# Reordered ends of the feed forward stages in a two-layer encoder on one core

## The chip, the cores and the metric

The kernel runs on one core of a Trainium2 chip. The metric is device time in microseconds (us) of one execution, the median of several runs. A core has a matmul engine (TensorE, PE in the rows; its weight loads are PEld), a vector engine (VectorE, DVE), a scalar engine (ScalarE, ACT), a general engine (GpSimd, POOL) and a sync engine (SyncE, SP) that issues most of the DMAs. Each takes its instructions in the order in which the program lists them and waits on semaphores. Matmul results land in PSUM, in banks that are reused; everything else sits in SBUF, 128 partitions wide.

## The reference, cut to what matters

The model is a two-layer bidirectional encoder of width 1024 over two request groups of 512 and 256 tokens, which the kernel holds together as 768 tokens. Each layer is a half feed forward stage, an attention mixer, and another half feed forward stage; a norm ends the whole.

```python
def _rmsnorm(x, g):
    xf = x.astype(jnp.float32)
    y = xf * lax.rsqrt(jnp.mean(xf * xf, axis=-1, keepdims=True) + NORM_EPS)
    return (y * g.astype(jnp.float32)).astype(x.dtype)

def _swiglu(h, wg, wu, wd):
    return (jax.nn.silu(h @ wg) * (h @ wu)) @ wd          # 1024 -> 2752 -> 1024
...
    for i in range(DEPTH):                                 # DEPTH = 2
        x = x + 0.5 * _swiglu(_rmsnorm(x, norm_ffn1[i]), ffn1_wg[i], ffn1_wu[i], ffn1_wd[i])
        h = _rmsnorm(x, norm_mix[i])
...
        x = x + 0.5 * _swiglu(_rmsnorm(x, norm_ffn2[i]), ffn2_wg[i], ffn2_wu[i], ffn2_wd[i])
    return _rmsnorm(x, final_norm)
```

## The kernel before, in words

The stages follow each other: feed forward (the first, to about 535 us), the mixer of layer 0, feed forward (the second, about 974 to 1486 us), feed forward (the third, 1486 to 1997 us), the mixer of layer 1, and the last feed forward stage (about 2369 us to the end). The first and the third stage hand over to a mixer, the second to the third.

Precision is kept by splitting every operand into a high and a low part, so that one product is three matmuls (`mm3h`: high times high, low times high, high times low). The activations stay transposed: `x` holds eight rows of 128 features (`j`) by 768 tokens, in two halves of 384 tokens.

**The up part** (`ffn_up`) computes gate and up projections. It starts with a leftover: three units for the first half of the tokens (`unit(0, i)`, 24 matmuls of 384 columns each, operands b11 and b21) and three for the second (`unit(1, i)`, operands b12 and b22). The second half needs its norm first. For that `rstd_cols` sums the squares `ss` by three small matmuls (L337), VectorE and GpSimd make the reciprocal root (L270, L271), and `norm_half` spreads it with two matmuls on a diagonal (`diag`, L354) and normalizes rows on VectorE (L310, then the low parts b12l and b22l at L307). These are placed by hand between the matmuls of the first half. Twenty tiles `t` follow, each a fast block scheme of seven products; `act_up` (L646) reads the last tile's PSUM.

**The down part** (`ffn_down`) is also seven products in a block scheme, in the order `DOWN = (1, 4, 5, 6, 7, 2, 0, 3)`; 0 stands for `rest(0)`, the leftover rows of the hidden width done the plain way for half of the tokens (40 matmuls), product 3 follows it, and then `rest(1)` closes the stage. A product has five quarters `q` of 24 matmuls. Its activations come from a queue `tu`: loaded from DRAM (`traw`, SyncE), cast to `th` on ScalarE (L766), and `tl` made as the difference on VectorE (L768); the tiles of all three come from one ring of nine. The weights come through a queue `gu` in the same way (`guh` on ScalarE L375, `gul` on VectorE L379; the leftover rows' at L184 and L189). `fetch(n)` has n loads on their way; `push(i, phases)` runs the cast, and with all phases the difference too, for the i-th operand in the queue; `ahead(0)` and `ahead(1)` do so in each quarter.

When a product has its sum in PSUM, `add` (L800, VectorE) takes two rows of it into `x`. In `rest` each finished row is handed on by `done(j, q)`: for a mixer `spread` (h_hi on ScalarE L277, h_lo on VectorE L278), for a next feed forward stage nothing of that, and for both `square` (ScalarE L285 or L288, summed into `ss` on VectorE L289) and `spill`, a DMA of the row on ScalarE's queue (L292). In the second stage `after` also runs parts of the third stage's norm within product 3 and `rest(1)`. In the last stage there is no `done`; `final` (`leave`) transposes a tile of 128 tokens back (L897), squares it on ScalarE (L900), gets the reciprocal root (L270, L271), multiplies by the gain on VectorE (L902), scales on ScalarE (L904) and sends it out (L905).

PSUM of the down part is a pool with tags `x` and `y`, two buffers each of two banks. Products 1, 6 and 7 build on one chain of two `y` buffers.

All of this is scheduled by hand: the order of the code is the order on each engine. The lines

```python
            if q == 0:
                tu.fetch(3)
            gu.fetch(1)
```

at the head of `rest`, and `ahead`, decide when operands are loaded and split relative to the adds and the rows handed on.

Of the kernel before, what the change touches and what calls it, by code (L numbers as in the profile page):

```python
# [17 lines left out]
KT = D // P  # L18
# [3 lines left out]
TT = T // P  # L22
# [113 lines left out]
class Kernel:  # L136
# [406 lines left out]
    def ffn_up(self, F, cpool, psp, gain, jobs):  # L543
        nc = self.nc
        x = self.xn
# [10 lines left out]
        def unit(q, i, ks=range(KT), ps=None):  # L556
            wh, wl = us[i]
            ps = ps or psum()
            for k in ks:
                w = slice(k * P, (k + 1) * P)  # L560
                bh, bl = (t[:, k % 4] for t in comb[f"b{k // 4 + 1}{q + 1}"])
                self.mm3h(ps[:, :TH], wh[:, w], wl[:, w], bh, bl, k == 0, k == KT - 1)
            return ps
# [22 lines left out]
        ps0 = [unit(0, 0)]  # L586
        if self.has_rc:
            self.norm_half(1, st, gain)
            ps0 += [unit(0, 1), unit(0, 2)]
        else:  # L590
            self.rstd_cols(st, range(TT // 2, TT), exact=False)
            ps = unit(0, 1, range(KT - 1))
            self.norm_half(1, st, gain)
            ps0.append(unit(0, 1, range(KT - 1, KT), ps))
            ps0.append(unit(0, 2))
        ps1 = [unit(1, i) for i in range(3)]
        prep0(0)
        sub(b(1, 1), b(1, 2), b(1, 1))
# [85 lines left out]
        with ExitStack() as cx:  # L684
            for t in range(self.NS):
                y, bb, c = psum(), psum(), psum()
# [97 lines left out]
    def ffn_down(self, F, ctx, done, after, final):  # L784
        nc = self.nc
        gu, tu, x = self.gu, self.tu, self.x
        NQ = self.NS // 4
        F.stash = ctx.enter_context(self.pool("stash", side=self.other()))
        psp = ctx.enter_context(self.psum_pool("dps", 2))
        new = lambda tag: psp.tile([P, 1024], F32, tag=tag, name=tag)  # L790
        def reload(i, q):
            for r, c in {1: [(0, 0)], 4: [(1, 0)], 5: [(1, 1), (0, 1)]}.get(i, []):
                if q < 4:
                    nc.sync.dma_start(out=x[:, 4 * r + q, HALVES[c]], in_=self.xscr[4 * r + q][:, HALVES[c]])

        def add(ps, js, c, w=TH, per=512):
            n = len(js)
            v = ps.rearrange("p (b c) -> p b c", c=per)[:, :n, :w]
            xs = x[:, js[0]:js[0] + n, c]
            nc.vector.scalar_tensor_tensor(out=xs, in0=v, scalar=0.5, in1=xs, op0=ALU.mult, op1=ALU.add)  # L800

        def ahead(part):
            if part == 0:
                tu.push(0)
                gu.push(1, 2)
                gu.push(2, 2)
                tu.fetch(2)
                gu.fetch(1)
            else:
                gu.push(1)  # L810
                tu.push(0)
                tu.push(1, 1)

        def product(i, banks, first):
            for q in range(NQ):
                (wh, wl), (th, tl) = gu.get(), tu.get()
                ahead(0)
                reload(i, q)
                if i == 1 and q < self.RAW:
                    a = F.stash.tile([P, 1024], F32, name=f"A{q}")  # L820
                    nc.scalar.copy(out=a, in_=F.A[q])
                    F.A[q] = a
                for j in range(4):
                    out = banks[j // 2][:, j % 2 * 512:j % 2 * 512 + TH]
                    for m in range(2):
                        w, c = slice(512 * m + P * j, 512 * m + P * j + P), slice(TH * m, TH * m + TH)
                        self.mm3h(out, wh[:, w], wl[:, w], th[:, c], tl[:, c], first and q + m == 0, q + m == NQ, not first)
                    if j % 2:
                        if q + 1 == NQ:
                            for r, c in self.ADDS[i]:  # L830
                                add(banks[j // 2], [4 * r + j - 1, 4 * r + j], HALVES[c])
                        if j == 1:
                            ahead(1)
                            yield 2 * q
                yield 2 * q + 1

        def rest(q):
            (wh, wl), (sh, _) = gu.get(), gu.get()
            (ah, al), (bh, bl) = tu.get(), tu.get()
            if q == 0:  # L840
                tu.fetch(3)
            gu.fetch(1)
            if q and final is not None:
                for i in range(TT // 2, TT):
                    ps = new("x")
                    c = slice(i * P - TH, i * P - TH + P)
                    for j in range(KT):
                        w, o = slice(j * P, (j + 1) * P), ps[:, j * P:(j + 1) * P]
                        self.mm3h(o, wh[:, w], wl[:, w], ah[:, c], al[:, c], True, False)
                        self.mm3h(o, sh[:, w], None, bh[:, c], bl[:, c], False, True)  # L850
                    add(ps, range(KT), slice(i * P, (i + 1) * P), P, P)
                    final(i, new("y"))
                return
            for j0 in range(0, KT, 2):
                ps = new("yyxx"[j0 // 2] if q == 0 else "xxyy"[j0 // 2])
                for j in (j0, j0 + 1):
                    w, o = slice(j * P, (j + 1) * P), ps[:, (j - j0) * 512:(j - j0) * 512 + TH]
                    self.mm3h(o, wh[:, w], wl[:, w], ah[:, :TH], al[:, :TH], True, False)
                    self.mm3h(o, sh[:, w], None, bh[:, :TH], bl[:, :TH], False, True)
                add(ps, (j0, j0 + 1), HALVES[q])  # L860
                if q and j0 == 2 and after is not None:
                    after(10, None)
                if j0 == 0:
                    gu.push(0)
                    gu.push(1, 2)
                    tu.push(0)
                elif j0 == 4:
                    gu.push(1)
                    gu.push(2, 2)
                if done is not None:  # L870
                    done(j0, q)
                    done(j0 + 1, q)
        chain = [new("y") for _ in range(2)]
        for i in self.DOWN:
            if i == 0:
                rest(0)
                continue
            banks = chain if i in (1, 6, 7) else [new("y" if i == 3 else "x") for _ in range(2)]
            for q in product(i, banks, i not in (6, 7)):
                if i == 3:  # L880
                    if final is not None:
                        if q in (3, 5, 7):
                            final((q - 3) // 2, new("x"))
                    elif after is not None:
                        after(q, lambda: new("x"))
        rest(1)

    def open_final(self, ctx, out):
# [1179 lines left out]
```

## Time and profile before

| | us |
|---|---|
| median of 3 timed runs | 2906.72 (2906.03 to 2907.74) |
| the profiled execution | 2897.25 |
| its span in the trace | 2895.2 |
| PE busy | 2724.2 (94%) |
| VectorE busy | 1985.8 (69%) |
| ScalarE busy | 1302.9 (45%) |

PE is the engine to look at: it is busy for nearly the whole span. What can be read is where it is not, and where the granted clock fell to half. In a row of a timeline the start is in us from the span's start, then the duration, engine, line, operation, output and inputs, and in brackets the idle time ahead of it and what ended that. Matmuls overlap, so the distance of two starts, not the duration, tells what one costs.

### The profile page before, as it was taken

What the parts mean: (1) busy time and instruction counts of PE and PEld (TensorE: products, weight loads), DVE (VectorE), ACT (ScalarE), POOL (GpSimd) and SP (SyncE); (2) the same over time, 40 slices, a digit from 0 to 9 for tenths busy, and PEclk for the clock granted to TensorE, in tenths of its full rate; (3) what the DMA queues carried; (4) which work ended last, traced back from release to release, by engine and by line L of the source; (5) the groups of instructions that cost most, each with busy time, mean ns of one, the idle gap of its engine ahead of it and who ended that gap; (6) DMA issues with size and microseconds to landing.
All of it is one profiled execution on the core that took longest, in us unless ns stands there. A gap on an engine that the chain in (4) does not pass through costs nothing. (4 is left out here: it accounts for less than half of the span.)

```text
span 2895.2 us, 41957 instructions
## 1 busy us (share of the span) xinstructions
PE 2724.2 (94%) x16118; PEld 2653.8 (92%) x16118; DVE 1985.8 (69%) x2902; ACT 1302.9 (45%) x2130; POOL 291.0 (10%) x428
## 2 busy tenths in 40 slices
PE   6999999998989999999989999998986899999997
PEld 6999998898978999999989999997985799999997
DVE  6777678454775676767887666686775558766684
ACT  4443344454675333334443333444566524333443
POOL 0000000032242000000000000000564400000000
PEclk9999999899999999999999999998998999999998
DMA  5474466358874243446534443654334243444652
GB/s 141 122 193 128 131 240 193 106 143 248 271 233 122 62 117 114 122 132 231 180 115 114 119 119 120 241 175 137 98 122 164 93 152 89 122 119 122 243 190 86
DMA packets 415656, 432.10 MB, mean 149 GB/s; under 512 B 34208, under 2 KB 353376, under 8 KB 414432
## 3 DMA queue, kind: packets, MB, share of 16 engines
q1 hardware_dynamic: 401632, 410.55, 46.8%
q10 hardware_dynamic: 13824, 18.88, 1.8%
q8 instruction: 126, 2.06, 0.3%
q14 instruction: 74, 0.61, 0.1%
HBM read 303.60 MB, written 125.76 MB: 148 GB/s over the span
## 5 line engine op out<-in xcount | busy, mean ns | idle before, releaser
L375 ACT CAST guh<-raw 128x1024 fp32r<-128x1024 f32 (+1 forms) x220 | 229.5, 1043 | 300.3 <-DVE raw L517 216.0
L379 DVE TENSOR_TENSOR gul<-raw,guh 128x1024 fp32r<-128x1024 f32 (+1 forms) x220 | 267.3, 1215 | 12.0 <-ACT guh L375 12.0
L477 PE MATMUL y<-th,guh 128*128 128x384 f32 x696 | 237.9, 342 | 21.0 <-ACT th L766 15.1
L477 PE MATMUL y<-tl,guh 128*128 128x384 f32 x696 | 237.0, 341 | 4.9 <-DVE tl L768 4.9
L477 PE MATMUL y<-th,gul 128*128 128x384 f32 x668 | 226.6, 339 | 0.0
L768 DVE TENSOR_TENSOR tl<-traw,th 128x768 fp32r<-128x768 f32 (+1 forms) x156 | 142.5, 914 | 92.9 <-ACT th L766 85.5
L477 PE MATMUL x<-tl,guh 128*128 128x384 f32 (+1 forms) x584 | 195.7, 336 | 6.1 <-DVE tl L768 6.1
L477 PE MATMUL x<-th,guh 128*128 128x384 f32 (+1 forms) x584 | 195.2, 336 | 1.8 <-DVE guh L184 1.8
L640 ACT COPY ap<-ps 128x384 f32<-128x384 f32 x160 | 77.0, 481 | 244.7 <-PE ps L477 244.6
L477 PE MATMUL x<-th,gul 128*128 128x384 f32 (+1 forms) x532 | 178.8, 336 | 0.0
L930 PE MATMUL pj<-guh,h_hi 128*128 128x256 f32 x576 | 168.8, 293 | 3.1 <-DVE x L800 3.0
L271 POOL TENSOR_TENSOR rc<-ms,expo 128x3 f32<-128x3 f32 (+1 forms) x10 | 10.2, 1015 | 1556.1 <-DVE ms L270 1556.1
L934 PE MATMUL pj<-guh,h_lo 128*128 128x256 f32 x576 | 166.2, 288 | 0.0
L933 PE MATMUL pj<-gul,h_hi 128*128 128x256 f32 x576 | 165.0, 287 | 0.0
L477 PEld LDWEIGHTS y<-th,guh 128*128 128x128 f32 x696 | 132.2, 190 | 24.7 <-ACT th L766 16.1
L477 PEld LDWEIGHTS y<-tl,guh 128*128 128x128 f32 x696 | 132.2, 190 | 7.0 <-DVE tl L768 7.0
L477 PE MATMUL ps<-b11l,guh 128*128 128x384 f32 x368 | 127.3, 346 | 7.3 <-DVE b11l L307 7.3
L766 ACT CAST th<-traw 128x768 fp32r<-128x768 f32 (+1 forms) x156 | 124.3, 797 | 20.4 <-DMA traw<-tq 14.0
L1051 POOL TENSOR_SCALAR p<-p,sm 128x256 f32<-128x256 f32 (+1 forms) x192 | 117.8, 625 | 137.6 <-DVE sm L1048 110.5
L477 PE MATMUL ps<-o,guh 128*128 128x384 f32 x512 | 131.2, 337 | 0.0
L646 DVE TENSOR_TENSOR act<-ps,g 128x384 f32<-128x384 f32 x80 | 44.6, 558 | 124.5 <-PE ps L477 118.9
L375 ACT CAST guh<-C 128x1024 fp32r<-128x1024 f32 x60 | 63.1, 1052 | 146.6 <-DVE C L450 96.7
(332 smaller groups left out, 8528.3 us busy)
## 6 DMA issues: line engine op xcount, KB each, us to landing
traw<-tq SPq DMA_DIRECT2D x140, 384.0 KB
raw<-in_ffn_wg_dram SPq DMA_DIRECT2D x84, 512.0 KB
raw<-in_ffn_wd_dram SPq DMA_DIRECT2D x80, 512.0 KB
rawu<-in_ffn_wu_dram SPq DMA_DIRECT2D x76, 512.0 KB
tq<-tl SPq DMA_DIRECT2D x80, 384.0 KB
xscr<-x ACTq DMA_DIRECT2D x96, 192.0 KB
tq<-act SPq DMA_DIRECT2D x40, 384.0 KB
x<-xscr SPq DMA_DIRECT2D x64, 192.0 KB
```

Of the source, the lines that this page charges most:

```text
L271: nc.gpsimd.tensor_tensor(out=self.rc[:, a:b], in0=ms[:, a:b], in1=self.expo[:, a:b], op=ALU.pow)
L375: self.nc.scalar.copy(out=hi, in_=raw)
L379: self.nc.vector.tensor_tensor(out=u[1], in0=raw, in1=f32(u[0]), op=ALU.subtract)
L477: mm = nc.tensor.matmul(out, w, x, start=start and n == 0, stop=stop and n == len(pairs) - 1, skip_group_check=more)
L640: nc.scalar.copy(out=c, in_=ps[:, :TH])
L646: tt(out=act[:, 0], in0=y[:, :TH], in1=g[:, 0], op=ALU.mult)
L766: nc.scalar.copy(out=th[:, :n], in_=t[:, :n])
L768: nc.vector.tensor_tensor(out=tl[:, :n], in0=t[:, :n], in1=f32(th[:, :n]), op=ALU.subtract)
L930: m = nc.tensor.matmul(out, self.h[:, k, s], wh[:, c], start=k == 0, stop=False)
L933: nc.tensor.matmul(out, self.h[:, k, s], wl[:, c], start=False, stop=False)
L934: nc.tensor.matmul(out, self.l[:, k, s], wh[:, c], start=False, stop=k == KT - 1)
L1051: nc.gpsimd.tensor_scalar(out=pt[:, c], in0=pt[:, c], scalar1=sm[:, 2 + s:3 + s], scalar2=1.0, op0=ALU.mult, op1=ALU.mult)
```

## The change

It alters five things, all in the feed forward stages.

1. In `ffn_up`, where the norm's reciprocal was not made beforehand (second, third and last stage), `rstd_cols` moves behind 12 more matmuls, and `norm_half` behind 9 more; the first half still ends at the same count of matmuls, so 18 instead of 27 stand between `norm_half` and the second half.
2. `ahead` gets the number of quarters left in products 2 and 3. With one left three loads are kept on their way instead of two; in the last quarter the second operand ahead is split in full (`tu.push(1, 9)`, so its `tl` too) before the second add.
3. `rest(0)` pushes the second activation operand of product 3 before its last add, and hands rows on later: two are kept back in a queue `late`, and the last two are handed on inside product 3.
4. The two `x` buffers of product 4 are taken before the chain's `y` buffers, so the chain lies in other banks.
5. In the last stage's `rest(1)` the transposes of a tile come after the matmuls of the next one.

```diff
@@ ffn_up
         else:
+            ps = unit(0, 1, range(KT // 2))
             self.rstd_cols(st, range(TT // 2, TT), exact=False)
-            ps = unit(0, 1, range(KT - 1))
+            ps0.append(unit(0, 1, range(KT // 2, KT), ps))
+            ps = unit(0, 2, range(2))
             self.norm_half(1, st, gain)
-            ps0.append(unit(0, 1, range(KT - 1, KT), ps))
-            ps0.append(unit(0, 2))
+            ps0.append(unit(0, 2, range(2, KT), ps))
@@ ffn_down
-        def ahead(part):
+        def ahead(part, left=9):
...
-                tu.fetch(2)
+                tu.fetch(3 if left == 1 else 2)
...
-                tu.push(1, 1)
+                tu.push(1, 9 if left == 0 else 1)
...
+                left = NQ - 1 - q if i in (2, 3) else 9
+                ahead(0, left)
...
-                            ahead(1)
+                            ahead(1, left)
@@ rest, with final
-                for i in range(TT // 2, TT):
+                for i in range(TT // 2, TT + 1):
+                    if i == TT:
+                        final(i - 1, new("y"))
+                        break
...
-                    final(i, new("y"))
+                    if i > TT // 2:
+                        final(i - 1, new("y"))
@@ rest, without
+                if q == 0 and j0 == 6:
+                    tu.push(1)
                 add(ps, (j0, j0 + 1), HALVES[q])
...
-                    done(j0, q)
-                    done(j0 + 1, q)
+                    late.extend((j0, j0 + 1))
+                    while len(late) > (0 if q else 2):
+                        done(late.popleft(), q)
+        late = deque()
+        spare = [new("x") for _ in range(2)]
         chain = [new("y") for _ in range(2)]
...
-            banks = chain if i in (1, 6, 7) else [new("y" if i == 3 else "x") for _ in range(2)]
+            banks = chain if i in (1, 6, 7) else spare if i == 4 else [new("y" if i == 3 else "x") for _ in range(2)]
...
                 if i == 3:
+                    if late:
+                        done(late.popleft(), 0)
```

VectorE in `rest(0)` of the first stage, from the end of the third block of rows on: L800 (L801 after) is an add, L278 and L289 are h_lo and ss of a row handed on, L379 is a weight's low part, L768 (L769 after) is the `tl` of a quarter of product 3. Before:

```order
L800 SCALAR_TENSOR_TENSOR x<-x 128x2x384
L278 SCALAR_TENSOR_TENSOR h_lo<-x,g_norm_mix_302,h_hi 128x384
L289 TENSOR_TENSOR ss<-ss,sq 128x384
L278 SCALAR_TENSOR_TENSOR h_lo<-x,g_norm_mix_302,h_hi 128x384
L289 TENSOR_TENSOR ss<-ss,sq 128x384
L768 TENSOR_TENSOR tl<-traw,th 128x768
L379 TENSOR_TENSOR gul<-A_3344,guh 128x1024
L768 TENSOR_TENSOR tl<-traw,th 128x768
```

After:

```order
L769 TENSOR_TENSOR tl<-traw,th 128x768
L801 SCALAR_TENSOR_TENSOR x<-x 128x2x384
L278 SCALAR_TENSOR_TENSOR h_lo<-x,g_norm_mix_302,h_hi 128x384
L289 TENSOR_TENSOR ss<-ss,sq 128x384
L278 SCALAR_TENSOR_TENSOR h_lo<-x,g_norm_mix_302,h_hi 128x384
L289 TENSOR_TENSOR ss<-ss,sq 128x384
L379 TENSOR_TENSOR gul<-A_3346,guh 128x1024
L278 SCALAR_TENSOR_TENSOR h_lo<-x,g_norm_mix_302,h_hi 128x384
L289 TENSOR_TENSOR ss<-ss,sq 128x384
L278 SCALAR_TENSOR_TENSOR h_lo<-x,g_norm_mix_302,h_hi 128x384
L289 TENSOR_TENSOR ss<-ss,sq 128x384
L769 TENSOR_TENSOR tl<-traw,th 128x768
```

The first `tl` (quarter 1 of product 3) moved from behind the last add and its rows to ahead of that add; four rows' h_lo and ss, where there were two, now stand between it and the `tl` of quarter 2.

PE at the start of the second stage, where the row sums (L337) stand among the first half's matmuls; ps_10047 is the PSUM of `unit(0, 0)`, ps_10078 (ps_10072 after) that of `unit(0, 1)`. Before:

```order
L477 MATMUL ps_10047<-b21h_9441,guh_10029 128x384
L477 MATMUL ps_10047<-b21l_9442,guh_10029 128x384
L477 MATMUL ps_10047<-b21h_9441,gul_10030 128x384
L337 MATMUL ps_10046<-ones2_71,ss_9447 128x2 x3
L477 MATMUL ps_10078<-b11h_9439,guh_10035 128x384
L477 MATMUL ps_10078<-b11l_9440,guh_10035 128x384
L477 MATMUL ps_10078<-b11h_9439,gul_10036 128x384
```

After:

```order
L477 MATMUL ps_10072<-b11h_9439,guh_10035 128x384
L477 MATMUL ps_10072<-b11l_9440,guh_10035 128x384
L477 MATMUL ps_10072<-b11h_9439,gul_10036 128x384
L337 MATMUL ps_10046<-ones2_71,ss_9447 128x2 x3
L477 MATMUL ps_10072<-b21h_9441,guh_10035 128x384
L477 MATMUL ps_10072<-b21l_9442,guh_10035 128x384
L477 MATMUL ps_10072<-b21h_9441,gul_10036 128x384
```

The sums moved from the border of the two units into the middle of the second one, 12 matmuls later.

PE at the very end, the last matmuls of the last block and the transposes of finished tiles (L897, L911 after). Before:

```order
L477 MATMUL x<-th,guh 128x128
L477 MATMUL x<-tl,guh 128x128
L477 MATMUL x<-th,gul 128x128
L477 MATMUL x<-th,guh 128x128
L477 MATMUL x<-tl,guh 128x128
L897 MATMUL y<-ident,x 128x128 x8
```

After:

```order
L477 MATMUL x<-th,guh 128x128
L477 MATMUL x<-tl,guh 128x128
L477 MATMUL x<-th,gul 128x128
L477 MATMUL x<-th,guh 128x128
L477 MATMUL x<-tl,guh 128x128
L911 MATMUL y<-ident,x 128x128 x16
```

Two groups of eight transposes stand behind the last matmul, where there was one.

## Rows read from the trace of the kernel before

**Rows 1.** The page's first part: busy us (share of the span) x instructions.

```profile
PE 2724.2 (94%) x16118; PEld 2653.8 (92%) x16118; DVE 1985.8 (69%) x2902; ACT 1302.9 (45%) x2130; POOL 291.0 (10%) x428
```

**Rows 2.** Timeline of PE, first stage's end: start, duration, instruction [idle <-releaser].

```profile
490.87 0.44 PE L477 MATMUL y<-tl,guh 128*128 128x384 f32 x1 [0.95 <-DVE tl L768]
...
501.05 0.33 PE L477 MATMUL y<-tl,guh 128*128 128x384 f32 x1
501.22 0.34 PE L477 MATMUL y<-th,gul 128*128 128x384 f32 x1
507.98 0.69 PE L477 MATMUL y<-th,guh 128*128 128x384 f32 x1 [6.42 <-ACT th L766]
508.97 0.69 PE L477 MATMUL y<-tl,guh 128*128 128x384 f32 x1 [0.31 <-DVE tl L768]
...
529.12 0.44 PE L477 MATMUL x<-tl,guh 128*128 128x384 f32 x1 [0.95 <-DVE tl L768]
```

**Rows 3.** Timeline of VectorE over the same end.

```profile
492.24 0.96 DVE L800 SCALAR_TENSOR_TENSOR x<-y,x 128x768 f32<-128x768 f32 x1 [1.42 <-PE y L477]
493.11 1.22 DVE L379 TENSOR_TENSOR gul<-A,guh 128x1024 fp32r<-128x1024 f32 x1
494.24 0.95 DVE L768 TENSOR_TENSOR tl<-traw,th 128x768 fp32r<-128x768 f32 x1
...
506.91 0.61 DVE L278 SCALAR_TENSOR_TENSOR h_lo<-x,g_norm_mix,h_hi 128x384 fp32r<-128x384 f32 x1
...
507.96 0.96 DVE L768 TENSOR_TENSOR tl<-traw,th 128x768 fp32r<-128x768 f32 x1
```

**Rows 4.** Timeline of PE where the down part begins, first and last stage.

```profile
362.78 0.45 PE L477 MATMUL y<-th,guh 128*128 128x384 f32 x1 [0.72 <-DVE act L646]
...
2701.23 0.45 PE L477 MATMUL y<-th,guh 128*128 128x384 f32 x1 [0.72 <-DVE act L646]
```

**Rows 5.** Windows at half clock: us, busy by engine (PE, PEld, DVE, ACT, POOL), PEclk, DMA.

```profile
505.96:512.79 6.83, 4.50 (x13) 4.10 (x14) 6.83 (x9) 5.34 (x8) 0.00 (x0) 0.50 0.28 95
...
1454.80:1458.20 3.40, 3.40 (x15) 3.39 (x13) 2.54 (x3) 1.79 (x3) 0.00 (x0) 0.51 0.66 214
...
1492.40:1495.90 3.50, 3.50 (x13) 3.50 (x14) 1.43 (x5) 0.00 (x0) 0.85 (x1) 0.51 0.80 251
...
2864.50:2874.70 10.20, 8.88 (x43) 8.70 (x43) 1.38 (x3) 1.11 (x2) 0.00 (x0) 0.50 0.00 0
```

**Rows 6.** Timeline of PE, ends of the second and the third stage.

```profile
1453.27 0.44 PE L477 MATMUL y<-th,guh 128*128 128x384 f32 x1 [2.46 <-ACT th L766]
...
1477.43 0.45 PE L477 MATMUL x<-tl,guh 128*128 128x384 f32 x1 [2.85 <-DVE tl L768]
...
1491.89 1.00 PE L337 MATMUL ps<-ones,ss 128*128 128x2 f32 x6 [1.70 <-DVE ss L289]
...
1969.52 0.69 PE L477 MATMUL y<-th,guh 128*128 128x384 f32 x1 [6.25 <-ACT th L766]
```

**Rows 7.** Timelines of VectorE and PE at the start of the second stage.

```profile
989.55 2.19 DVE L310 SCALAR_TENSOR_TENSOR x<-x,g_norm_ffn,ps 128x384 f32<-128x384 f32 x4 [1.66 <-PE ps L354]
...
995.49 1.94 DVE L307 TENSOR_TENSOR b22l<-x,b22h 128x768 fp32r<-128x768 f32 x2
...
994.03 0.34 PE L477 MATMUL ps<-b12h,guh 128*128 128x384 f32 x1
```

**Rows 8.** Timelines of PE and ScalarE in the last stage's closing rows.

```profile
2863.25 0.33 PE L477 MATMUL x<-tl,guh 128*128 128x128 f32 x1 [1.07 <-DVE tl L768]
...
2871.33 1.97 PE L897 MATMUL y<-ident,x 128*128 128x128 f32 x8 [1.32 <-DVE x L800]
...
2887.84 1.02 ACT L900 ACTIVATE ysq<-y 128x1024 f32<-128x1024 f32 x1 [2.93 <-PE y L897]
...
2890.40 1.33 ACT L904 ACTIVATE y<-y,rc 128x512 f32<-128x512 f32 x2 [1.45 <-POOL rc L271]
```

**Rows 9.** Timeline of ScalarE, a weight cast that waits for its load.

```profile
472.84 1.05 ACT L375 CAST guh<-raw 128x1024 fp32r<-128x1024 f32 x1 [2.80 <-DMA raw<-in_ffn_wd_dram]
```

More of the change, by code (lines that the diff above doesn't have):

```diff
@@ L816, in product @@
                 (wh, wl), (th, tl) = gu.get(), tu.get()
-                ahead(0)
+                left = NQ - 1 - q if i in (2, 3) else 9
+                ahead(0, left)
                 reload(i, q)
```

## The prediction

> **What bounds the kernel now.** I read the engines' busy shares first, then the matmul engine's timeline where it stands idle, then VectorE's timeline over the same stretches, then the windows with the granted clock. PE is busy for 94% of the span [rows 1], so an edit is worth what it takes from PE's gaps, from its half-clock stretches, or adds to them. All four feed forward stages have the same gaps, and nearly all lie where the change puts its hands.
>
> The end of the first stage shows them [rows 2]. PE waits 0.95 us for the second leftover operand's low part (490.87). It issues the last leftover matmul at 501.22 and the first of product 3 at 507.98, where full speed is one per 0.17 us (501.05 to 501.22): 6.76 - 0.17 = 6.59 us gone, put down to the ScalarE cast of `th`. At 508.97 it waits again for `tl`, and at 529.12 0.95 us more, in the last leftover rows. Counted start to start, this end loses 1.15 + 6.59 + 0.67 + 1.14 = 9.55 us.
>
> Who is late there is VectorE [rows 3]. Each `add` holds the next instruction back by 0.87 us (492.24 to 493.11), a `gul` by 1.13 (493.11 to 494.24), a pair of h_lo and ss by 1.05 (506.91 to 507.96); `tl` of 768 columns is as long as an `add`. From 492.24 on, four adds, two gul, one tl and eight such pairs stand ahead of the `tl` of product 3's second quarter (3.5 + 2.3 + 0.9 + 8.4 = 15.1), which therefore starts only at 507.96, just as PE's long wait ends. The ScalarE cast is held by the same interleaving, since the rows' casts stand before it.
>
> Two more kinds of gap: when a stage goes from its up to its down part PE waits 0.72 us for `act_up` to leave a bank; the first and the last of four such rows are shown [rows 4]. And PE runs at half clock (1.2 GHz, granted 0.50 or 0.51) for 6.8 us after the 6.42 us wait, for 10.2 us in the last rows, and for three stretches of about 3.4 us at the end of the second stage, of which the first and the last stand in [rows 5].
>
> **The change part by part.** The order of the changed kernel moves instructions and adds none, so each part is costed as an arrival against a completion.
>
> *Banks.* The y chain gets the banks that the last up tile does not read. 4 x 0.72 = **-2.9**. Bounds: 0, if another late reader stands in the new banks, to -4 x 0.89 start to start.
>
> *Ends of the first and third stages.* Second leftover operand before the second add: the wait of 490.87 falls away, and so does the one of 529.12, for the `tl` now ends one add earlier (0.87). Then VectorE's queue, walked with [rows 3] from the first add at 491.1 (1.15 sooner than 492.24): ahead of the `tl` of quarter 1 stand now three adds, two gul, one tl and three and a half pairs: 2.6 + 2.3 + 0.9 + 3.5 = 9.3, so with its own 0.95 it ends at about 501.3. PE, 1.15 sooner than 501.22 + 0.17, arrives at 500.2: 1.0 waited. Then one add, four pairs, one gul and one tl: 0.87 + 4.2 + 1.1 + 0.95 = 7.1, so the `tl` of quarter 2 is there at about 508.2 while PE, 24 matmuls of 0.173 on, wants it at 505.5: 2.7 waited. Quarter 3 comes 2.1 us later against 4.2 of matmuls and waits for nothing. Left 3.7 of 9.55: **-5.8**. In the third stage the wait is 6.25 [rows 6]: **-5.5**. Bounds for each: -9.5, if ScalarE's casts let the rows pass without idling VectorE, to -3, if the half-microsecond waits for h_hi come on top of each remaining row. The rows handed on later carry their spill DMAs on ScalarE's queue with them, one or two rows later; what is queued behind these are casts of later quarters, and nobody reads the spilled rows before the next stage, so I cost them at nothing; without that cover it would be one issue each on ScalarE, before a `th` that is early. SyncE's order of loads is the same in both kernels. The next stage's start is held by the last add in both and moves with it.
>
> *End of the second, start of the third stage* [rows 6]. Waits of 2.46, 2.85 and 1.70 (the last for `ss` at the row sums) and, like those of [rows 2], one of 0.95 and one of some 0.6 for `tl` are removed or moved: 8.6, counted start to start 8.8. The statistics stand 12 matmuls (2.1 us) later, but PE also arrives earlier, by the waits that are gone. Walking VectorE's queue with the durations of [rows 3, 7], I leave 1.2 still for `ss`, 0.8 for the diag (18 matmuls of cover where there were 21), 2.7 for banks that the last add and L310 free, and 1.7 for the second half's operands. 8.8 - 6.4: **-2.4**; bounds 0 and -4.
>
> *Statistics later in the second and last stages.* There was no gap to remove here [rows 7]. After the diag matmuls come L310 (989.55) and the halves' splits; the first b22l is written at 995.49 + 0.97 = 996.46. PE starts the second half at 994.03 and wants b22l 13 matmuls later, at 996.28: no slack. The diag now stands 9 matmuls (1.56 us) later while the second half starts at the same place, so this chain comes late by that: +1.5 twice, **+3.0**. Bounds 0, if VectorE catches up in the splits, and +4.
>
> *Last stage.* Its first leftover wait goes as in the first stage: **-0.9**. In the tail [rows 8] the wait of 1.07 for the second operand shrinks by an add, -0.9. Transposes after the next block's matmuls hide two waits of 1.32 and take one group of about 1.0 behind the last block: the last matmul comes 3.6 earlier. But ScalarE now has two tiles in a row behind it, each 3.9 us from its square (2887.84) to the end of its scaling (2890.40 + 1.33), and the last tile starts one such chain after the one before it instead of 1.3 after the block: 2.6 given back. Tail **-1.9**; bounds -0.8 and -3.7.
>
> *Clock* [rows 5]. A half-clock stretch loses what it lets lie: 13 matmuls in 6.83 us are 2.3 us lost, and half of 3.4 us is 1.7. The gaps before the falls were 6.42, 2.46, 2.85 and 1.70 [rows 2, 6]; none stands after one of 1.32 [rows 8]. The first and third ends keep a gap of 2.7, so I leave one stretch of 3.4 in each: -0.6 and -0.4. The second end loses 4.8 in three stretches, and I leave one: -3.1. Sum **-4.1**; bounds 0, and -9.5 when none is left.
>
> The rows put a fall behind a gap of only 1.70. In the Trainium skill, "TensorE: Matmul & The Clock Gate", section "HAM oscillation — how this bites in real kernels" ties the fall to idle gaps above a bound that no gap which I leave reaches. By that rule the stretches at these ends would all go, and the sum would be about 5 us lower; the rows at 1.70, 2.46 and 2.85 speak against it here, so I don't follow it.
>
> **Sum.** -2.9 - 5.8 - 5.5 - 2.4 + 3.0 - 0.9 - 1.9 - 4.1 = -20.5. The terms come from the one profiled execution (span 2895.2, run 2897.25); the median of the timed runs, 2906.72, is 9.5 above it, and I take this distance as unchanged: 2906.7 - 20.5 = **2886**.
>
> **Rivals.**
> 1. The clock is kept. If the shortened gaps no longer drop it, 5.4 more is gained at the ends, and the tail, no more at half clock, gives up to 1.8 and a little at the next stage's start: about 2878. For it: no stretch follows the gap of 1.32. Against: 1.70 did. That is also what the rule of the page named above would give. Chance 0.13.
> 2. VectorE is the bound and the wait only moves into product 3. It is busy for all of 6.83 us in the window at 505.96 [rows 5], and its work isn't reduced. Then only the banks (-2.9), the leftover operands (-0.9 four times and -1.0 twice), the tail (-1.9) and the statistics (+3.0) count: -7.4, 2899. Against: product 3 gives VectorE 4.2 us per quarter and asks 2.1. Chance 0.09.
> 3. The moved instructions are covered again by other waits (a bank with a late reader, a queue that stands): nothing comes of it, 2907. Chance 0.04.
> 4. Slower: the third operand fetched ahead takes tiles of the ring of nine, so the load for a later quarter is issued only when the first leftover operands are let go. A load issued late costs PE its flight: ScalarE waited 2.80 for one [rows 9], plus its issue, 3.4. Two per end in four ends: 27, less the 20 gained: 2913. It decides from 1.5 late loads per end on. Against: the tiles are free when the leftover matmuls end at about 500 and the fourth quarter is wanted some ten microseconds later. Chance 0.05.
> The main case has 0.69.
>
> **How the numbers follow.** The main case's own range: without clock (+4.1), stalls 3 worse, tail 1.1 worse: 2894; bounds the other way about 2877. Rivals 1 and 2 are taken in, and a microsecond at either side: 2876 to 2900; 3 and 4 and the ends of the main case stay outside. A measurement of this kernel tells some 0.2% (5.8 us) from no change. Faster: 0.67 of the main case, 0.13, and 0.05 of rival 2: 0.85. Same: 0.02 + 0.04 + 0.04 = 0.10. Slower 0.05.
>
> **What would show it.** Right: no 0.72 wait at the four changes to the down part; no wait of 0.95 in the leftover rows; at the first end about 1 us before quarter 1 and 2 to 3 us before quarter 2, for `tl`, in place of 6.42; new waits of about 1.5 for b22l at the starts of the second and the last stage; two transposes groups in a row at the very end, with ScalarE the last engine. Wrong: a wait for DMA on `traw`; half clock at the second end in three stretches as before; or the wait before quarter 2 as long as 6 us.

## The result and the profile after

The changed kernel took 2874.66 us (median of 4 runs, 2872.42 to 2876.99) where the kernel before took 2907.23: a ratio of 0.9889, interval 0.9877 to 0.9901. That is 32.6 us less; 20.5 were forecast, and the time lies 1.3 us under the range. A second measurement (after_again, below) gave 2878.37 us, which lies inside it: 0.9918 (0.9902 to 0.9934), 25.5 us less. The two profiled executions differ by 24.6 us (2895.2 to 2870.6).

PE of the changed kernel (the page's first part: busy us, share of the span, instructions) stands beside [rows 1]:

```profile
PE 2716.7 (95%) x16118; PEld 2646.1 (92%) x16118; DVE 1985.3 (69%) x2902; ACT 1301.5 (45%) x2130; POOL 292.0 (10%) x428
```

The timeline of PE, at the first stage's end and the mixer behind it, the second stage's start, the third stage's first unit and the third stage's end:

```profile
500.81 0.45 PE L477 MATMUL y<-tl,guh 128*128 128x384 f32 x1 [0.77 <-DVE tl L769]
...
507.68 0.45 PE L477 MATMUL y<-tl,guh 128*128 128x384 f32 x1 [2.40 <-DVE tl L769]
...
531.75 0.42 PE L1340 MATMUL pc<-gul,h_hi 128*128 128x336 f32 x1 [2.62 <-DVE gul L189]
...
986.22 0.44 PE L477 MATMUL ps<-b12l,guh 128*128 128x384 f32 x1 [0.60 <-DVE b12l L307]
...
988.14 0.44 PE L477 MATMUL ps<-b22l,guh 128*128 128x384 f32 x1 [0.59 <-DVE b22l L307]
...
1472.78 0.41 PE L477 MATMUL ps<-b11h,guh 128*128 128x384 f32 x1 [1.71 <-DVE x L801]
...
1941.29 0.44 PE L477 MATMUL y<-tl,guh 128*128 128x384 f32 x1 [0.59 <-DVE tl L769]
...
1948.15 0.44 PE L477 MATMUL y<-tl,guh 128*128 128x384 f32 x1 [2.36 <-DVE tl L769]
```

Against [rows 2] and [rows 6], the waits of 6.42 and 6.25 us have become 0.77 and 2.40 at the first end and 0.59 and 2.36 at the third; 0.95, 2.46 and 2.85 are gone, and so are the four of 0.72 of [rows 4]. New are the pairs of 0.6 us for b12l and b22l at the starts of the second, third and last stage. VectorE shows why it is 0.77 and 2.40: the two `tl` of product 3 that PE waits for now start at 499.81 and 506.67, with an add, four pairs of h_lo and ss and a gul between them (the first of the two started at 507.96 in [rows 3]).

```profile
499.81 0.95 DVE L769 TENSOR_TENSOR tl<-traw,th 128x768 fp32r<-128x768 f32 x1
500.68 0.95 DVE L801 SCALAR_TENSOR_TENSOR x<-x 128x768 f32<-128x768 f32 x1
...
506.67 0.95 DVE L769 TENSOR_TENSOR tl<-traw,th 128x768 fp32r<-128x768 f32 x1
```

Windows (us; busy time of PE, PEld, DVE, ACT, POOL; PEclk; DMA share; GB/s) show the clock at the places of [rows 5]: full at all three ends in this execution, half in the tail, and there for 20.5 us where it was 10.2.

```profile
488.00:531.00 43.00, 37.78 (x213) 36.19 (x211) 36.26 (x50) 25.92 (x42) 0.00 (x0) 1.00 0.52 161
...
1438.00:1504.00 66.00, 60.91 (x341) 58.37 (x340) 59.63 (x81) 31.33 (x43) 2.29 (x2) 1.00 0.44 122
...
1930.00:1972.00 42.00, 36.89 (x209) 35.73 (x207) 35.08 (x48) 25.23 (x42) 0.00 (x0) 1.00 0.51 167
...
2834.00:2854.50 20.50, 20.18 (x94) 20.02 (x95) 4.29 (x7) 1.11 (x2) 0.00 (x0) 0.50 0.07 23
```

The tail is the last stage's `rest(1)` to the end of the kernel. PE waits at its start for `tl` and for the low part of the second leftover weight, which L184 writes into half of its `guh`, and no longer 1.32 us behind each block:

```profile
2832.06 0.33 PE L477 MATMUL x<-tl,guh 128*128 128x128 f32 x1 [1.10 <-DVE tl L769]
...
2834.27 0.45 PE L477 MATMUL x<-th,guh 128*128 128x128 f32 x1 [1.77 <-DVE guh L184]
...
2859.48 1.09 PE L911 MATMUL y<-ident,x 128*128 128x128 f32 x8 [0.42 <-DVE x L801]
```

### The profile page after: what moved, and what is told of

Its sections match the earlier page's. It is cut to its first block, busy times and chain, and to the rows that moved or that the text cites. A ratio compares the mean times of both kernels' runs of the same rounds, so it can differ in the third digit from the quotient of the medians.

```text
span 2870.6 us, 41973 instructions
## 1 busy us (share of the span) xinstructions
PE 2716.7 (95%) x16118; PEld 2646.1 (92%) x16118; DVE 1985.3 (69%) x2902; ACT 1301.5 (45%) x2130; POOL 292.0 (10%) x428
## 5 line engine op out<-in xcount | busy, mean ns | idle before, releaser
L379 DVE TENSOR_TENSOR gul<-raw,guh 128x1024 fp32r<-128x1024 f32 (+1 forms) x220 | 267.4, 1215 | 12.0 <-ACT guh L375 12.0
L769 DVE TENSOR_TENSOR tl<-traw,th 128x768 fp32r<-128x768 f32 (+1 forms) x156 | 142.6, 914 | 87.9 <-ACT th L767 86.4
L477 PEld LDWEIGHTS y<-tl,guh 128*128 128x128 f32 x696 | 130.6, 188 | 10.2 <-DVE tl L769 10.2
```

What stands on the lines that cost most here:

```text
L379: self.nc.vector.tensor_tensor(out=u[1], in0=raw, in1=f32(u[0]), op=ALU.subtract)
L477: mm = nc.tensor.matmul(out, w, x, start=start and n == 0, stop=stop and n == len(pairs) - 1, skip_group_check=more)
L769: nc.vector.tensor_tensor(out=tl[:, :n], in0=t[:, :n], in1=f32(th[:, :n]), op=ALU.subtract)
```

## The experiments

Times are medians; the ratios are to the kernel before, run on the same chip in the same job. The undone parts are shown against the changed kernel.

**The kernel before again, and the changed kernel again.**

> The kernel before once more, for its trace and for the clock of several runs. Theory A (the 10 us between the profiled execution of before, 2897.25, and its timed median, 2907, are half-clock time of TensorE): the runs near 2907 show a mean granted clock of about 0.969 to 0.970 where the profiled one had 0.973, that is some 20 us more at half speed, and these stretches lie in stages that were at full clock in the first trace. Theory B (they lie outside the clock: loads or launch): clock 0.973 in all runs, spans of about 2905 us, and the added time is in gaps of PE.

Measured: 2904.84 us over 12 executions (ratio 0.9994, 0.9984 to 1.0005), but these lie between 2894 and 2911, with mean clocks of 0.968 to 0.973. The profiled execution of the first measurement, 2897.25, is one of the shorter ones among them. Clock and time go together only loosely (2900.6 us of span at 0.969, 2905.3 at 0.971), so theory A holds in direction and not in size. Where it does hold can be seen in the tail, in the windows from the tail's first wait to the end, of the first trace of before and of this one:

```profile
2859.60:2895.20 35.60, 21.28 (x143) 20.31 (x143) 11.18 (x14) 8.73 (x15) 1.63 (x3) 0.76 0.18 59
```

```profile
2854.30:2899.70 45.40, 31.07 (x143) 29.85 (x143) 11.20 (x14) 8.75 (x15) 1.63 (x3) 0.55 0.14 47
```

The same instructions take 35.6 us in one and 45.4 in the other, at mean clocks of 0.76 and 0.55: as much as the whole distance of 9.5 us that the prediction carried along as unchanged. The two spans differ by only 4.5 us (2895.2 and 2899.7), so elsewhere this execution was the shorter one. And the wait of 1.70 us that stood ahead of a half-clock stretch in [rows 5, 6] stands here too, with full clock behind it:

```profile
1489.61 0.83 PE L337 MATMUL ps<-ones,ss 128*128 128x2 f32 x6 [1.70 <-DVE ss L289]
```

```profile
1489.60:1493.00 3.40, 3.39 (x22) 3.39 (x23) 1.43 (x5) 0.00 (x0) 0.86 (x1) 1.00 0.87 268
```

> The changed kernel once more beside the variants, for its time on the same chip and a second trace. Theory 1 (the gain beyond the forecast is clock that stays up at the ends of the first three stages): no half-clock stretch at these ends again, waits for tl of about 0.8 and 2.4 in product 3, a half-clock stretch of about 20 us in the tail, time 2872 to 2877. Theory 2 (the clock at these ends was luck of the first trace): one or more stretches of 3.4 us stand at the ends, and the time scatters up to 2880.

Measured: 2878.37 us (2869.58 to 2883.26). Both theories hold in part. The waits of product 3 and of the second end are the same to 0.02 us, the second end is again without half clock, but a stretch of 3.4 us stands behind the waits of 2.4 at the first and third end (windows of PE behind these two waits):

```profile
509.60:513.00 3.40, 3.40 (x12) 3.40 (x12) 3.40 (x4) 0.00 (x0) 0.00 (x0) 0.51 0.28 71
...
1946.70:1950.10 3.40, 3.40 (x12) 3.40 (x11) 3.40 (x4) 0.00 (x0) 0.00 (x0) 0.50 0.37 90
```

**Part 3 undone** (no early push and no late rows in `rest(0)`).

```diff
-                if q == 0 and j0 == 6:
-                    tu.push(1)
...
-                    late.extend((j0, j0 + 1))
-                    while len(late) > (0 if q else 2):
-                        done(late.popleft(), q)
+                    done(j0, q)
+                    done(j0 + 1, q)
```

> The changed kernel without its part 3 (rest(0) splits no operand of product 3 ahead of its last add and hands rows on at once). Theory 1 (the long waits of product 3 for its th come from the order of VectorE and ScalarE around the rows handed on): waits of about 6 us stand again before product 3 in the first and third stage and of about 2.5 in the second, half clock follows each, and the time is 2874.7 plus 6 + 6 + 3 and some 6 of clock, about 2893 to 2896. Theory 2 (VectorE's total work is the bound, the order moves the wait only): about 2877 to 2880.

Measured: 2893.03 us, 0.9956 (0.9944 to 0.9968). Theory 1. The waits of the kernel before are back to the hundredth, and 10.2 us of half clock stand at the first and at the second end (PE's timeline, and the window at the first end):

```profile
507.34 0.69 PE L477 MATMUL y<-th,guh 128*128 128x384 f32 x1 [6.42 <-ACT th L767]
...
1453.17 0.69 PE L477 MATMUL y<-th,guh 128*128 128x384 f32 x1 [2.46 <-ACT th L767]
```

```profile
503.80:514.00 10.20, 6.35 (x19) 5.96 (x20) 8.94 (x11) 6.04 (x9) 0.00 (x0) 0.50 0.54 178
```

Against the changed kernel's two medians this part carries 15 to 18 us of the change, and 13 to 20 if each is counted from the kernel before in its own job.

**Part 2 undone** (`tu.fetch(2)`, `tu.push(1, 1)` in `ahead`).

> The changed kernel without part 2 (second leftover operand split after the second add again, no third load ahead). Theory 1 (its waits of 0.95 add to the time): they stand again in both leftover parts of the first three stages and in the first of the last, about 1 us each, 6 to 8 us slower, about 2884. Theory 2 (VectorE is late anyway, so a wait of 0.95 ahead is taken off the tl waits of 0.8 and 2.4 behind it): the first leftover parts cost nothing, only the second ones do, 2 to 4 us slower, about 2880.

Measured: 2886.13 us, 0.9943 (0.9929 to 0.9958), 8 to 11 us behind the changed kernel's two medians. Theory 1, and more than it asked: besides the waits of 0.95 us the one of 2.85 at the second end is back, with half clock behind it, and the waits of 0.77 and 2.40 behind the first 0.95 have not shrunk, which theory 2 wanted (PE's timeline, first and second end):

```profile
490.72 0.45 PE L477 MATMUL y<-tl,guh 128*128 128x384 f32 x1 [0.95 <-DVE tl L769]
502.34 0.44 PE L477 MATMUL y<-tl,guh 128*128 128x384 f32 x1 [0.77 <-DVE tl L769]
509.20 0.44 PE L477 MATMUL y<-tl,guh 128*128 128x384 f32 x1 [2.40 <-DVE tl L769]
...
1469.96 0.45 PE L477 MATMUL x<-tl,guh 128*128 128x384 f32 x1 [2.86 <-DVE tl L769]
```

That fits the dependence: VectorE's first add needs PE's block, so a wait ahead of the block delays VectorE's whole queue by as much.

**Part 4 undone** (no `spare`).

> The changed kernel with the order of the banks as before. Theory 1: the wait of 0.72 for act_up stands again at the four changes from the up to the down part, each such stretch is 0.9 longer, 3 to 3.6 us slower than the changed kernel, about 2880. Theory 2 (the wait is hidden by another at the same place): no such wait or no difference in the stretch.

Measured: 2879.49 us, 0.9918 (0.9902 to 0.9935). Theory 1 by the trace: the 0.72 is back, as here at the first change to the down part, and each such stretch is about 1 us longer. In time it is not told apart from the changed kernel.

```profile
361.95 0.44 PE L477 MATMUL y<-th,guh 128*128 128x384 f32 x1 [0.72 <-DVE act L647]
```

**Part 1 undone, in all stages and in two of three.** In u_stats the old order stands in all three stages; in m_stats the new one only where a feed forward stage hands over to another:

```diff
-        else:
+        elif self.handed:
             ps = unit(0, 1, range(KT // 2))
...
+        else:
+            self.rstd_cols(st, range(TT // 2, TT), exact=False)
+            ps = unit(0, 1, range(KT - 1))
...
+            k.handed = n > 0 and stages[n - 1][0] == "f"
```

> The changed kernel with the statistics and the diagonal where they stood before in all three stages. Theory 1 (this part costs 1.6 us each at the starts of the second and last stage, where nothing waited for ss, by waits for b12l and b22l of 0.6 each and their tails): these four waits go, 3.2 us are gained; at the third stage's start a wait for ss at L337 of up to 1.7 comes back. Time 2871.5 to 2873.2. Theory 2 (the later statistics are what keeps the clock up at the third stage's start): the wait for ss returns with half-clock stretches, 2876 to 2878.

> The changed kernel with part 1 kept at the third stage's start only and undone at the second and the last. Theory 1 (at those two the later statistics cost 1.2 to 1.6 us each in waits for b12l and b22l; at the third they save a wait for ss of 1.7 and the half clock behind it): 2.4 to 3.2 us below the changed kernel in the same job, and u_stats's loss comes from the third stage alone. Theory 2 (the two waits of 0.6 are hidden later): no difference.

Measured: u_stats 2878.62 us, 0.9909 (0.9895 to 0.9924); m_stats 2877.92, 0.9912 (0.9895 to 0.9929), where the changed kernel had 2878.37 in m_stats's job. In u_stats the four waits of 0.6 are gone, but at the third stage's start a wait of 3.57 us stands, twice what was expected, because PE comes there earlier than in the kernel before, and half clock behind it (PE's timeline and a window):

```profile
1476.68 0.80 PE L337 MATMUL ps<-ones,ss 128*128 128x2 f32 x6 [3.57 <-DVE ss L289]
```

```profile
1477.80:1481.20 3.40, 3.40 (x12) 3.40 (x11) 1.27 (x4) 0.00 (x0) 0.86 (x1) 0.50 0.56 185
```

So theory 2 is the nearer one there. In m_stats no wait for b12l or b22l is left at the second and last stage, and 72 matmuls from the first of the second half on take 13.0 us at the second and 12.8 at the last stage, where both traces of the changed kernel have 14.6 and 14.3: the price is there in the trace, 1.6 us each, but the time shows no gain among executions that scatter by 14 us.

**Part 5 undone, and part 5 alone on the kernel before** (transposes right behind each block, or behind the next one).

```diff
-                    if i > TT // 2:
-                        final(i - 1, new("y"))
+                    final(i, new("y"))
```

> The changed kernel with the last stage's transposes right behind each block again. Theory 1 (staggering hides two waits of 1.32 and gives back 2.6 in ScalarE's chain): 1 us slower, 2875.7. Theory 2 (the staggered order keeps TensorE at half clock for 20 us of the tail where it was 10, and costs more than it hides): the half-clock stretch of the tail is 10 us again and the time 2 to 4 us shorter, 2871 to 2873.

> The kernel before with part 5 of the change alone (transposes after the next block's matmuls). Theory 1 (without staggering the tail is at half clock for 31 to 43 us in most executions, the 19 us of the first trace being rare; staggering keeps it at 20.5 plus 8): 5 to 7 us faster than before, about 2899, and a tail of 30 to 31 us from the first matmul of rest(1) to the last. Theory 2 (the tail's clock is random in both orders): 1 to 2 us faster, as the waits alone give.

Measured: u_tail 2880.54 us, 0.9912 (0.9899 to 0.9926); only_tail 2902.29, 0.9991 (0.9978 to 1.0004). The first looked like 6 us for this part; the second, with 12 executions, gives 1.6, with an interval from 6.4 us faster to 1.2 slower. From the tail's first matmul to the end the staggered order took 39 to 44 us in eight traces (mean 40.3) and the other 36, 45 and 46 in three; in both, half clock begins at the tail's first waits and lasts between 10 and 44 us. Staggering removes the waits of 1.32, as forecast; it doesn't keep the clock up. Whether it shortens the half-clock stretch on average, three traces can't tell.

**What decides the tail's clock.** In m_sh both leftover operands and the second weight are split ahead of the first add in the last quarter; m_sh3 also runs `final` a quarter earlier in product 3, so that its squares and products don't stand before these casts; m_best is m_sh3 with m_stats.

```diff
-                gu.push(1, 2)
+                gu.push(1, 9 if left == 0 else 2)
+                if left == 0:
+                    tu.push(1)
...
-                        if q in (3, 5, 7):
-                            final((q - 3) // 2, new("x"))
+                        if q in (1, 3, 5):
+                            final((q - 1) // 2, new("x"))
```

> The changed kernel with a mended start of the last stage's rest(1): final runs half a quarter earlier in product 3, and in its last quarter both leftover operands and the second leftover weight are split in full before the first add, in all stages. Theory 1 (the waits of 1.10 and 1.77 us at the start of the last stage's rest(1) drop the clock for the tail): both waits go or fall under 0.6, the tail stays at full clock or falls later, 2.4 of waits and 5 to 9 of clock gained, 2861 to 2867 where the changed kernel has 2874. Theory 2 (the tail's clock falls whatever these waits are, since blocks of 128 columns and waits for adds follow): 2 to 3 us gained, 2871 to 2873.

> As m_sh3 but with final at its old place in product 3: only the second leftover weight and operand are split before the first add. Theory 1 (the tail's clock falls after the waits at the start of rest(1), which final's ScalarE and VectorE work still causes here): waits of about 1.1 for tl and 1.3 for the weight stay, the tail falls to half clock for 17 to 30 us again, 2871 to 2877. Theory 2 (the wait of 1.77 for the weight alone drops the clock): the tail stays at full clock, 2865 to 2868.

> The changed kernel with both mends: the start of the last rest(1) as in m_sh3, and the statistics later at the third stage's start only. Theory 1 (the two mends add): the waits for b12l and b22l of 0.6 at the starts of the second and last stage go (1.4 to 1.7 us each by the traces of m_stats), the tail stays at full clock: 2861 to 2863, where m_sh3 had 2865. Theory 2 (what the statistics save there is lost to clock elsewhere, as in m_stats's time): 2864 to 2866.

Measured: m_sh3 2865.27 us, 0.9869 (0.9853 to 0.9885); m_sh 2874.56, 0.9891 (0.9875 to 0.9907); m_best 2867.45, 0.9870 (0.9856 to 0.9883). The waits at the tail's start, and the tail's windows, of m_sh3 and then of m_sh:

```profile
2835.96 0.33 PE L477 MATMUL x<-th,guh 128*128 128x128 f32 x1 [0.71 <-ACT th L767]
2836.55 0.33 PE L477 MATMUL x<-tl,guh 128*128 128x128 f32 x1 [0.27 <-DVE tl L769]
```

```profile
2835.90:2852.00 16.10, 15.36 (x134) 14.98 (x135) 7.27 (x8) 2.89 (x6) 0.55 (x1) 1.00 0.08 22
```

```profile
2832.49 0.33 PE L477 MATMUL x<-tl,guh 128*128 128x128 f32 x1 [1.25 <-DVE tl L769]
2833.85 0.33 PE L477 MATMUL x<-th,guh 128*128 128x128 f32 x1 [0.92 <-ACT th L767]
```

```profile
2834.90:2863.00 28.10, 28.10 (x134) 28.10 (x134) 6.19 (x7) 2.93 (x5) 0.54 (x1) 0.50 0.10 31
```

134 matmuls take 16.1 us behind waits of 0.71 and 0.27, and 28.1 behind waits of 1.25 and 0.92 (and one of 0.26). From its first matmul the whole tail takes 27.9 us in m_sh3 and 27.7 in m_best, 42.6 in m_sh and 38.7 in after_again. Theory 1 holds in both: waits of hardly more than 1 us each, close to one another at the tail's start, cost some 12 us of clock. m_sh3 beats both kernels, by 13 us the changed one in its job. m_best adds nothing that its 4 executions show. The mend did not remove all waiting: it moved a wait for `tl` some 5 us ahead, among the 384-column matmuls of product 3, and the clock stayed full behind it in both traces, even behind 1.74 us (m_sh3, then m_best):

```profile
2830.68 0.44 PE L477 MATMUL y<-tl,guh 128*128 128x384 f32 x1 [0.93 <-DVE tl L769]
```

```profile
2834.20 0.45 PE L477 MATMUL y<-tl,guh 128*128 128x384 f32 x1 [1.74 <-DVE tl L775]
```

So the size of one wait does not decide alone; what else does was not separated.

## Why the prediction was wrong

The direction and most of the waits were right, the clock was not.

Distances between the same two matmuls in each trace, in us, show where the time went. The first column has their starts in the first trace of before; the forecast of an end has its share of the clock term in it.

| stretch | before, b_again | after, after_again | forecast |
|---|---|---|---|
| first end, 488.2 to 549.2 | 61.0, 61.5 | 53.8, 55.4 | -6.4 |
| second end, 1437.1 to 1520.6 | 83.6, 82.1 | 75.2, 75.2 | -5.5 |
| third end, 1950.1 to 2010.1 | 60.0, 60.6 | 53.0, 54.5 | -5.9 |
| tail, from 2859.15 to the end | 36.0, 46.0 | 39.9, 38.7 | -1.9 |
| mixer of layer 0, 549.2 to 960.1 | 410.9, 409.6 | 409.3, 408.1 | 0 |

The three ends gave 22.6 us in the first pair of traces and 19.1 in the second, for 17.8 forecast; the tail became 3.9 longer in the first pair and 7.2 shorter in the second.

*Right, step by step.* Banks: -2.9 forecast; the four waits of 0.72 are gone, and the stretches around them are about 1 us shorter each. Product 3: 1.0 and 2.7 us of waiting forecast, 0.77 and 2.40 measured at the first end. Statistics: +1.5 at each of two stages forecast, 1.6 by the trace of m_stats. The mixer's first wait, taken as held by the last add, is 2.62 for the low part of the mixer's own first weight instead; that costs the same, since the stretch from the last leftover matmuls to the mixer's norm (L335) is 14.0 us before and after. Leftover operands: the waits of 0.95 are gone.

*Mis-sized: the waits at the second end.* 6.4 us were left there; measured are 1.17 for `ss`, 0.59 and 1.71 for banks, 0.60 and 0.59 for b12l and b22l, 4.7 in all. The diag never waits. At the tail's start 0.9 was to be saved: the second operand's wait of 1.07 is gone, but the first one's, 0.29 before, is 1.10.

*Wrong: the clock term.* The step was "the rows put a fall behind a gap of only 1.70", and one stretch was left at each end on its strength: -4.1 of a possible -9.5. The changed kernel shows none in the first trace and two in the second. That row was the exception: with the same wait of 1.70 the second trace of before stays at full clock, and behind the waits of 1.5 to 1.7 at the third stage's start (1472.78 above) none of the nine traces that have one shows a fall. But a shorter wait can do it too. Behind the 1.17 us for `ss` in the second stage's product 3 the clock fell in two of ten traces, u_banks and u_ahead; here is u_banks:

```profile
1442.71 0.80 PE L337 MATMUL x<-ones,ss 128*128 128x2 f32 x6 [1.17 <-DVE ss L289]
```

```profile
1443.80:1447.20 3.40, 3.40 (x13) 3.40 (x12) 3.37 (x7) 0.28 (x1) 1.43 (x1) 0.50 0.64 171
```

For waits of 2.4 the step was about right: in the ten traces with part 3 the clock fell behind them in 7 at the first end and in 5 at the third, though not in the trace that was measured first. So rival 1, with chance 0.13, is what the first trace shows at the ends, and something between it and the main case is the rule. By the rule in the Trainium skill, "TensorE: Matmul & The Clock Gate", section "HAM oscillation — how this bites in real kernels", no single gap of this size would drop the clock. The 12 falls of 20 contradict that here, and so does the tail.

*Wrong: the tail's clock and the distance of 9.5 us.* The tail of the first trace of before was read as typical, with 10.2 us at half clock. b_again has 31.6 us of it ahead of its last wait. So the profiled execution was a short one of a kernel that scatters, and the distance to the median was no constant to carry along. From its first matmul to the end the tail got 3.9 us longer between the two first traces, against -1.9 forecast, but b_again's tail is 46.0. One such tail is enough to turn 24.6 us between two traces into 32.6 between two medians; that it was this one in the timed runs of before is inferred, since these have no trace, and b_again's own execution, 2901.81, is with such a tail still under its median. Both kernels scatter by 14 to 17 us, so what of the 32.6 is the change's own stays open by some microseconds: two measurements gave 32.6 and 25.5. A part of the scatter lies where no kernel here differs: the same matmuls of the mixer of layer 0 take 407.7 to 412.5 us in the fourteen traces. These are the shortest (u_banks) and the longest (u_late):

```profile
542.70:950.40 407.70, 380.79 (x2695) 360.46 (x2696) 234.30 (x480) 226.54 (x527) 113.55 (x222) 0.97 0.63 187
```

```profile
548.50:961.00 412.50, 385.04 (x2695) 365.02 (x2696) 234.81 (x480) 226.83 (x527) 114.25 (x222) 0.96 0.62 185
```

*The range* was too narrow for the same reason: it was drawn from the terms with one microsecond to spare, after three timed runs that lay within 1.7 us, where twelve of b_again lie within 17.

*Rivals 2 and 4.* VectorE's queue gave product 3 what was counted: the stall did not move further in. None of PE's waits in product 3 is put down to a load in any trace, so no cost of the third operand's load shows.

## What to carry to other kernels

Walk the late engine's queue with durations from the trace: it gave the remaining waits of product 3 to 0.4 us, and the order of instructions, with nothing removed, was worth some 15 us in one part. But take the clock term from more than one execution, since the same wait drops the clock in one and not in the next. And read what an edit is worth between the same two instructions before and after, which keeps the scatter of the rest out. And look for waits of a microsecond close together, as at the tail's start here: removing them from there was worth another 13 us against the changed kernel in the same job.

## What the runs showed of the hardware

Behind waits of 2.36 to 2.43 us in product 3 the granted clock fell to 0.50 for 3.4 us in 12 of 20 cases; the two traces of the changed kernel differ in this with one and the same program and the same waits. Behind 1.17 us for `ss` it fell in 2 of 10, behind 1.5 to 1.7 at the third stage's start in 1 of 12, and behind the 3.6 us for b11l, which open the second and the last stage in every kernel, in 28 of 28:

```profile
977.85 0.69 PE L477 MATMUL ps<-b11l,guh 128*128 128x384 f32 x1 [3.63 <-DVE b11l L307]
```

In the tail it fell behind a pair of waits of 1.25 and 0.92 us, and in all eleven traces with one of 1.77, which has another of 0.6 to 1.2 close by; it then stayed at half for 10 to 44 us although PE was busy for most of it (28.10 of 28.10 us in m_sh). With 0.71 and 0.27 it stayed full until PE's work was done.
